# Input projection of a hybrid SSD and attention layer: seven Strassen products summed in three PSUM banks in place of seven

## The chip, the cores and the metric

The kernel runs on one core of one Trainium2 chip. The metric is the device time of one execution in microseconds (us). The core's engines work side by side, each through its own queue in order: TensorE (PE in the profile, its weight loads PEld), VectorE (DVE), ScalarE (ACT), GpSimd (POOL), and SyncE (SP), which here only issues transfers.

## The reference, cut to what matters

One decoder layer over 1024 tokens and 1024 channels. The normalised input `h` goes through one wide input projection, and its columns feed a Mamba-2 (SSD) branch, a causal attention branch with a forget gate, and two gates. The branches are projected, gated, summed and projected once more.

```python
h = _rmsnorm(x, norm_w) * (1.0 + scale[:, None, :]) + shift[:, None, :]
proj = jnp.einsum("bsd,de->bse", h, w_in)
z_ssm, xbc, dt_raw, q, k, v, z_att, f_logit, g_logit = jnp.split(proj, offsets, axis=-1)
y_ssm = _ssd_branch(z_ssm, xbc, dt_raw, ...)      # silu(conv(xbc)), decay sums, states, norm
y_att = _fox_branch(q, k, v, z_att, f_logit, b_f)
g_ssm, g_att = jnp.split(jax.nn.sigmoid(g_logit + b_gate), N_BRANCHES, axis=-1)
merged = g_ssm * (y_ssm @ w_proj_ssm) + g_att * (y_att @ w_proj_att)
x = x + gate[:, None, :] * (merged @ w_out)
return _rmsnorm(x, final_norm_w)
```

The change touches the columns of `w_in` that give `z_ssm`, `xbc`, `z_att` and 12 of the 16 blocks of 128 columns of `g_logit`: 38 blocks of 128 columns, worked off as 19 pairs.

## The kernel before, in words

`h` is kept transposed (channels on the partitions). Every float32 product is made of three single-pass matmuls: each operand is split into a rounded part (hi) and a remainder (lo), and hi*hi + hi*lo + lo*hi are added in PSUM. A split of a weight tile is a cast on ScalarE (line 102) and a subtraction on GpSimd (line 103).

Stages in time: start-up (`h` itself, the first three gate blocks), one block of values with the dt and forget columns, the sums of `h` that Strassen's scheme needs (`t_forms`), the decay sums (`dt_chain`), then the 19 slab pairs (some 120 to 540 us of the span), then the SSD stage with the rest of the projection as filling, the attention, and three more projections.

A slab pair (`c_pair`, lines 459 to 518) computes two blocks of 128 output channels for all 1024 tokens by Strassen's scheme in Winograd's form: seven products f1 to f7 in place of eight. Each product is 12 matmuls of 128x512 (four k blocks by three terms) into a PSUM bank of 128x512 float32. There are eight banks, three under the tag `mm` and five under `pp`. The weights of a pair come as four raw tiles by DMA (buffers: four, shared with other loads). VectorE makes the sums S1, S2, A11-A21 and S4 (lines 477 to 480). Then seven splits follow.

The products are added up outside TensorE. With P1 to P7 the products in the order f1, f6, f7, f5, f4, f2, f3, before the change:

- P1 is copied to SBUF as x1 (ScalarE, line 503)
- VectorE makes u2 = P6 + x1 (504), u3 = P7 + u2 (505), u4 = P5 + u2 (507), and adds in the bank P5 + u3 (508), P4 + u3 (511), P2 + x1 (514), P3 + u4 (517)
- the four banks with results are evacuated by the functions of the two slabs: a tanh on ScalarE for a gate (line 186), a tanh and a VectorE multiply for z (524, 525), a ScalarE copy into a padded tile for the convolution (534)

After a pair of convolution blocks, VectorE runs five instructions of 128x1024 for each of the two blocks (lines 538, 541, 544, with a tanh on ScalarE, line 543, before the last), and the result is stored (line 545). Convolution pairs are numbers 1, 3, 5, 7 and 9 of the 19, counted from 0. Between the pairs stand side jobs by the table `WPREP`: `w_sums` (four more raw tiles, VectorE sums at lines 586 and 587, GpSimd at 588 and 589, stores), and `out_gate` (32 VectorE instructions in all, lines 558 and 561).

The order on each engine is not written out by hand. The framework schedules the instructions on a model of the engines, by program order as priority, and then each queue is fixed. A queue is first in, first out: an instruction that waits holds up everything behind it. All transfers stand in SP's queue.

## Time and profile before

| | |
|---|---|
| three timed runs | 1295.77, 1300.94, 1301.15 us; median 1300.94 us |
| span of the profiled execution | 1298.8 us |
| time of the profiled execution around its span | not listed apart; the span is 2.1 us under the median |
| PE busy | 1204.0 us, 93% |
| DVE busy | 986.1 us, 76% |
| POOL, ACT busy | 775.3 us, 589.6 us |
| matmuls | 6206 |
| moved by DMA | 219.69 MB |

The busy time of an engine is an average over stages. Whether an engine binds in a stage is read from windows of that stage: how many matmuls start in a window, what TensorE's clock was, and what TensorE waited for where it stood idle. The granted clock has two levels, 1.2 and 2.4 GHz; the profile gives it as a share of full speed, averaged over a window.

### The profile page before, as it was taken

What the parts mean: (1) busy time and instruction counts of PE and PEld (TensorE: products, weight loads), DVE (VectorE), ACT (ScalarE), POOL (GpSimd) and SP (SyncE); (2) the same over time, 40 slices, a digit from 0 to 9 for tenths busy, and PEclk for the clock granted to TensorE, in tenths of its full rate; (3) what the DMA queues carried; (4) which work ended last, traced back from release to release, by engine and by line L of the source; (5) the groups of instructions that cost most, each with busy time, mean ns of one, the idle gap of its engine ahead of it and who ended that gap; (6) DMA issues with size and microseconds to landing.
All of it is one profiled execution on the core that took longest, in us unless ns stands there. A gap on an engine that the chain in (4) does not pass through costs nothing. (4 is left out here: it accounts for less than half of the span.)

```text
span 1298.8 us, 18747 instructions
## 1 busy us (share of the span) xinstructions
PE 1204.0 (93%) x6206; PEld 998.6 (77%) x6206; DVE 986.1 (76%) x1673; ACT 589.6 (45%) x1184; POOL 775.3 (60%) x644
## 2 busy tenths in 40 slices
PE   4897999999978999999998999999999899999896
PEld 3686788777766888899877888888888787878684
DVE  6979777787799565259889854545666968999997
ACT  5543333333342322567666633444456463444354
POOL 3267556475665565457887857435446645687666
PEclk9998899999989999999999999999998999999998
DMA  8432433633565566753744548623236618756143
GB/s 345 155 125 72 167 114 130 210 114 114 186 231 191 186 219 226 234 163 119 230 120 155 195 164 299 212 84 116 72 132 202 199 53 318 245 169 192 51 119 140
DMA packets 100669, 219.69 MB, mean 169 GB/s; under 512 B 11434, under 2 KB 19036, under 8 KB 99548
## 3 DMA queue, kind: packets, MB, share of 16 engines
q1 hardware_dynamic: 100572, 218.50, 50.4%
q8 instruction: 49, 0.80, 0.2%
q14 instruction: 48, 0.39, 0.1%
HBM read 154.85 MB, written 63.61 MB: 168 GB/s over the span
## 5 line engine op out<-in xcount | busy, mean ns | idle before, releaser
L103 POOL TENSOR_TENSOR wl<-wr,wh 128x512 fp32r<-128x512 f32 (+1 forms) x188 | 284.5, 1523 | 137.1 <-ACT wh L102 129.6
L102 ACT CAST wh<-wr 128x512 fp32r<-128x512 f32 (+1 forms) x214 | 129.7, 618 | 161.3 <-DMA wr<-w_c 51.7
L103 POOL TENSOR_TENSOR sl<-sr,sh 128x512 fp32r<-128x512 f32 x57 | 91.2, 1607 | 79.1 <-ACT sh L102 59.5
L116 PE MATMUL mm<-hl,wh 128*128 128x512 f32 x288 | 117.9, 409 | 2.9 <-DVE hl L307 2.9
L115 PE MATMUL mm<-hh,wh 128*128 128x512 f32 x288 | 116.6, 410 | 4.3 <-ACT wh L102 2.0
L117 PE MATMUL mm<-hh,wl 128*128 128x512 f32 x288 | 117.0, 407 | 0.0
L140 PE MATMUL mm<-wh,hh 128*128 128x256 f32 (+1 forms) x256 | 74.8, 294 | 3.9 <-DVE tmp L348 3.9
L102 ACT CAST sh<-sr 128x512 fp32r<-128x512 f32 x57 | 34.1, 619 | 97.1 <-DVE sr L478 77.9
L141 PE MATMUL mm<-wl,hh 128*128 128x256 f32 (+1 forms) x256 | 74.6, 292 | 0.0
L142 PE MATMUL mm<-wh,hl 128*128 128x256 f32 (+1 forms) x256 | 74.4, 291 | 0.0
L1014 ACT ACTIVATE pr<-pr,sm 128x1024 f32<-128x1024 f32 (+3 forms) x64 | 49.9, 780 | 51.5 <-DVE sm L1013 43.9
L1017 POOL TENSOR_SCALAR pr<-pr,sm 128x1024 f32<-128x1024 f32 (+3 forms) x64 | 49.3, 772 | 38.1 <-DVE sm L1016 31.8
L1009 DVE CUSTOM_DVE_ANT_0 pr<-lg,fb 128x512 f32<-128x512 f32 (+1 forms) x96 | 51.6, 551 | 25.1 <-PE lg L1008 14.6
L115 PEld LDWEIGHTS mm<-hh,wh 128*128 128x128 f32 x288 | 55.4, 194 | 16.2 <-ACT wh L102 2.4
L116 PEld LDWEIGHTS mm<-hl,wh 128*128 128x128 f32 x288 | 56.0, 194 | 15.3 <-DVE hl L307 3.9
L117 PEld LDWEIGHTS mm<-hh,wl 128*128 128x128 f32 x288 | 55.9, 194 | 11.3
L1000 POOL TENSOR_SCALAR_AFFINE_SELECT fb<-fb 128x128 f32<-128x128 f32 x64 | 20.6, 323 | 70.1 <-DVE sm L1009 57.2
L1033 DVE TENSOR_TENSOR ptl<-tp,pth 128x512 fp32r<-128x512 f32 (+1 forms) x80 | 50.1, 632 | 15.0 <-ACT pth L1032 14.1
L1032 ACT CAST pth<-tp 128x512 fp32r<-128x512 f32 (+1 forms) x80 | 42.4, 544 | 41.8 <-PE tp L1029 32.8
L684 ACT ACTIVATE ab<-ab,acs 128x128 f32<-128x128 f32 x128 | 41.2, 391 | 28.9 <-DMA ab<-a_scr 28.8
L140 PEld LDWEIGHTS mm<-wh,hh 128*128 128x128 f32 x256 | 49.3, 193 | 5.1 <-DVE tmp L348 4.6
L103 POOL TENSOR_TENSOR m<-ab,m 128x512 fp32r<-128x512 f32 x32 | 47.2, 1475 | 7.2 <-ACT m L102 6.8
(394 smaller groups left out, 3989.3 us busy)
## 6 DMA issues: line engine op xcount, KB each, us to landing
wr<-w_c SPq DMA_DIRECT2D x116, 256.0 KB, 3.6
wa<-w_ada SPq DMA_DIRECT2D x8, 1024.0 KB, 11.4
g_scr<-gt SPq DMA_DIRECT2D x16, 512.0 KB, 3.9
ab<-a_scr SPq DMA_DIRECT2D x32, 256.0 KB, 3.8
gt<-g_scr SPq DMA_DIRECT2D x32, 256.0 KB, 3.2
wr<-w_ps SPq DMA_DIRECT2D x28, 256.0 KB, 2.7
wr<-w_pa SPq DMA_DIRECT2D x28, 256.0 KB, 3.0
wr<-so SPq DMA_DIRECT2D x28, 256.0 KB, 2.7
```

The costliest lines, as they stand in the source:

```text
L102: A.copy(out=hi[:, :n], in_=raw[:, :n])
L103: eng.tensor_tensor(out=lo[:, :n], in0=raw[:, :n], in1=f32(hi[:, :n]), op=ALU.subtract)
L115: PE.matmul(ps, lhsT=hi[:, cs], rhs=xh[k][:, hs], start=(k == 0), stop=False)
L116: PE.matmul(ps, lhsT=hi[:, cs], rhs=xl[k][:, hs], start=False, stop=False)
L117: PE.matmul(ps, lhsT=lo[:, cs], rhs=xh[k][:, hs], start=False, stop=(k == 7))
L140: PE.matmul(o, lhsT=xh[k][:, ts], rhs=hi[:, cs], start=(k == 0), stop=False)
L141: PE.matmul(o, lhsT=xh[k][:, ts], rhs=lo[:, cs], start=False, stop=False)
L142: PE.matmul(o, lhsT=xl[k][:, ts], rhs=hi[:, cs], start=False, stop=(k == 7))
L1009: V.tensor_tensor_reduce(out=pr[:, n0:n1], in0=lg[:, :n1 - n0], in1=fb[:, n0:n1], op0=ALU.add, op1=ALU.min, scale=1.0, scalar=BIG, accum_o ...
L1014: A.activation(out=pr[:, :n], in_=pr[:, :n], func=AF.Exp, scale=-1.0, bias=sm[:, 0:1], accum_out=sm[:, 1:2])
L1017: G.tensor_scalar(out=pr[:, :n], in0=pr[:, :n], scalar1=sm[:, 1:2], scalar2=0.5, op0=ALU.mult, op1=ALU.mult)
L1033: V.tensor_tensor(out=ptl[:, :w], in0=tp[:, :w], in1=f32(pth[:, :w]), op=ALU.subtract)
```

## The change

The seven products of a pair now take three banks. `prod` gets an optional bank: given one, none of its 12 matmuls starts a new sum, and they add to what stands there.

- bank a: P1; copied to x1; then P2 is added by TensorE: this is the first result
- bank b: P6; VectorE adds x1 in place (line 509); copied to u2 by ScalarE (510); then P7 is added by TensorE; copied to u3 by ScalarE (513); then P4 is added: the second result
- bank d: P5; VectorE writes P5 + u3 to an SBUF tile c22 (516), which is the third result, and adds u2 in place (517); then P3 is added: the fourth result

So VectorE's seven additions become three, ScalarE's one copy becomes three, and four additions are done by matmuls that were there before. The number of matmuls is the same. The products are now issued as f1, f6, f5, f7, f2, f4, f3, and the splits as f1, f6, f5, f7, f2, f4, f3. The evacuation of the third result reads SBUF, not PSUM. Comments are removed throughout the file, so lines from 499 on move by one to four.

```diff
@@ -480,42 +480,46 @@
             f1 = a_form(a11)
             f6 = s_form(s2)
+            f5 = s_form(s1)
             f7 = a_form(a21)
-            f5 = s_form(s1)
+            f2 = a_form(a12)
             f4 = a_form(a22)
-            f2 = a_form(a12)
             f3 = s_form(s4)
 
-            def prod(f, xs, k0, hf):
-                ps = bank()
+            def prod(f, xs, k0, hf, ps=None):
+
+                first, ps = ps is None, bank() if ps is None else ps
...
-                    PE.matmul(ps, lhsT=f[0][:, w], rhs=xh[:, hs], start=(k == 0), stop=False)
...
+                    PE.matmul(ps, lhsT=f[0][:, w], rhs=xh[:, hs], start=(first and k == 0), stop=False,
+                              skip_group_check=True)
...
-            x1, u2, u3, u4 = pe_tile(), pe_tile(), pe_tile(), pe_tile()
-            A.copy(out=x1, in_=prod(f1, h, 0, 0))
-            V.tensor_tensor(out=u2, in0=prod(f6, ttb, 0, 1), in1=x1, op=ALU.add)
-            V.tensor_tensor(out=u3, in0=prod(f7, tta, 0, 1), in1=u2, op=ALU.add)
-            ps = prod(f5, tta, 0, 0)
-            V.tensor_tensor(out=u4, in0=ps, in1=u2, op=ALU.add)
-            V.tensor_tensor(out=ps, in0=ps, in1=u3, op=ALU.add)
-            evac_b(hi, ps)
-            ps = prod(f4, ttb, 0, 0)
-            V.tensor_tensor(out=ps, in0=ps, in1=u3, op=ALU.add)
-            evac_b(lo, ps)
-            ps = prod(f2, h, 4, 0)
-            V.tensor_tensor(out=ps, in0=ps, in1=x1, op=ALU.add)
-            evac_a(lo, ps)
-            ps = prod(f3, h, 4, 1)
-            V.tensor_tensor(out=ps, in0=ps, in1=u4, op=ALU.add)
-            evac_a(hi, ps)
+
+            x1, u2, u3, c22 = pe_tile(), pe_tile(), pe_tile(), pe_tile()
+            pa_ = prod(f1, h, 0, 0)
+            A.copy(out=x1, in_=pa_)
+            pb = prod(f6, ttb, 0, 1)
+            V.tensor_tensor(out=pb, in0=pb, in1=x1, op=ALU.add)
+            A.copy(out=u2, in_=pb)
+            pd = prod(f5, tta, 0, 0)
+            prod(f7, tta, 0, 1, pb)
+            A.copy(out=u3, in_=pb)
+            prod(f2, h, 4, 0, pa_)
+            evac_a(lo, pa_)
+            V.tensor_tensor(out=c22, in0=pd, in1=u3, op=ALU.add)
+            V.tensor_tensor(out=pd, in0=pd, in1=u2, op=ALU.add)
+            prod(f4, ttb, 0, 0, pb)
+            evac_b(lo, pb)
+            evac_b(hi, c22)
+            prod(f3, h, 4, 1, pd)
+            evac_a(hi, pd)
```

Three places show how the scheduled order moves. The numbers behind names are buffer numbers; `cv` and `xp` are the convolution's tiles, `sr` sums of weights, `gb` the out_gate row.

VectorE, the end of convolution pair 9, before (`mm_3139`, `mm_3155`, `pp_3170`, `pp_3185` are four products of pair 10):

```order
L505 TENSOR_TENSOR pe_3095<-mm_3125,pe_3094 128x512
L541 SCALAR_TENSOR_TENSOR cv_3008<-xp_2848,cols_80,cv_3008 128x1024
L507 TENSOR_TENSOR pe_3096<-mm_3139,pe_3094 128x512
L544 SCALAR_TENSOR_TENSOR cv_3000<-xp_2846,cv_3000 128x1024
L508 TENSOR_TENSOR mm_3139<-mm_3139,pe_3095 128x512
L511 TENSOR_TENSOR mm_3155<-mm_3155,pe_3095 128x512
L586 TENSOR_TENSOR sr_3380<-wr_3374,wr_3376 128x512
L544 SCALAR_TENSOR_TENSOR cv_3008<-xp_2848,cv_3008 128x1024
L514 TENSOR_TENSOR pp_3170<-pp_3170,pe_3093 128x512
L587 TENSOR_TENSOR sr_3381<-sr_3380,wr_3372 128x512
L517 TENSOR_TENSOR pp_3185<-pp_3185,pe_3096 128x512
```

The same place on VectorE now (`mm_3066` is bank d of pair 10, `mm_3211` bank b of pair 11):

```order
L545 SCALAR_TENSOR_TENSOR cv_2940<-xp_2792,cols_80,cv_2940 128x1024
L545 SCALAR_TENSOR_TENSOR cv_2948<-xp_2794,cols_80,cv_2948 128x1024
L545 SCALAR_TENSOR_TENSOR cv_2940<-xp_2792,cols_80,cv_2940 128x1024
L545 SCALAR_TENSOR_TENSOR cv_2948<-xp_2794,cols_80,cv_2948 128x1024
L590 TENSOR_TENSOR sr_3308<-wr_3302,wr_3304 128x512
L548 SCALAR_TENSOR_TENSOR cv_2940<-xp_2792,cv_2940 128x1024
L591 TENSOR_TENSOR sr_3309<-sr_3308,wr_3300 128x512
L548 SCALAR_TENSOR_TENSOR cv_2948<-xp_2794,cv_2948 128x1024
L516 TENSOR_TENSOR pe_3036<-mm_3066,pe_3035 128x512
L517 TENSOR_TENSOR mm_3066<-mm_3066,pe_3034 128x512
L509 TENSOR_TENSOR mm_3211<-mm_3211,pe_3193 128x512
```

The additions of the pair in flight stood between the convolution's instructions; now they stand behind them, and the addition that bank b of pair 11 needs is the last.

ScalarE at the same place, before:

```order
L543 ACTIVATE xp_2848<-cv_3008 128x1024
L503 COPY pe_3259<-pp_3263 128x512
L102 CAST wh_3432<-wr_3417 128x512
L186 ACTIVATE gt_3049<-mm_3139,cols_80 128x512
L186 ACTIVATE gt_3049<-mm_3155,cols_80 128x512
L186 ACTIVATE gt_3048<-pp_3170,cols_80 128x512
```

ScalarE at the same place now:

```order
L547 ACTIVATE xp_2794<-cv_2948 128x1024
L513 COPY pe_3035<-pp_3051 128x512
L507 COPY pe_3193<-mm_3197 128x512
L102 CAST wh_3360<-wr_3345 128x512
L510 COPY pe_3194<-mm_3211 128x512
L186 ACTIVATE gt_2988<-pp_3037,cols_80 128x512
L186 ACTIVATE gt_2989<-pp_3051,cols_80 128x512
```

The copy of u2 of pair 11 (line 510) stands behind a cast of a freshly loaded raw tile, in the place where the gate evacuations of pair 10 stood.

TensorE, where product f7 of pair 5 ends, before (f5 follows, into another bank):

```order
L495 MATMUL pp_2216<-tha3_1134,wh_2164 128x512
L496 MATMUL pp_2216<-tla3_1135,wh_2164 128x512
L497 MATMUL pp_2216<-tha3_1134,wl_2165 128x512
L495 MATMUL pp_2230<-tha0_1062,sh_2168 128x512
L496 MATMUL pp_2230<-tla0_1063,sh_2168 128x512
```

TensorE at the end of product f7 of pair 5 now:

```order
L496 MATMUL mm_2172<-tha3_1134,wh_2138 128x512
L498 MATMUL mm_2172<-tla3_1135,wh_2138 128x512
L499 MATMUL mm_2172<-tha3_1134,wl_2139 128x512
L496 MATMUL mm_2172<-thb0_1064,wh_2146 128x512
L498 MATMUL mm_2172<-tlb0_1065,wh_2146 128x512
```

Here f4 follows f7 in the same bank with nothing between, so the copy of u3 must be made between two matmuls. In the other 18 pairs 10 to 30 matmuls of other products stand between f7 and f4, and 21 to 67 between f6 and f7 in all 19.

## Rows read from the trace of the kernel before

**Rows 1.** The head of the profile page: the span, and busy time, share and instructions of TensorE and VectorE.

```profile
span 1298.8 us, 18747 instructions
...
PE 1204.0 (93%) x6206; PEld 998.6 (77%) x6206; DVE 986.1 (76%) x1673; ACT 589.6 (45%) x1184; POOL 775.3 (60%) x644
```

**Rows 2.** Stretches of 50 us: length, then busy us of each engine with the number of instructions, TensorE's clock, the DMA share and GB/s.

```profile
100.00:150.00 50.00, 41.69 (x169) 33.29 (x167) 47.03 (x68) 17.86 (x34) 33.31 (x23) 0.84 0.25 78
...
150.00:200.00 50.00, 50.00 (x217) 40.57 (x216) 34.01 (x38) 17.54 (x28) 29.75 (x20) 1.00 0.44 149
...
250.00:300.00 50.00, 44.43 (x186) 34.10 (x184) 34.96 (x44) 16.00 (x28) 30.23 (x18) 1.00 0.45 152
300.00:350.00 50.00, 46.24 (x189) 36.33 (x190) 38.07 (x43) 21.18 (x37) 32.75 (x21) 0.97 0.40 134
350.00:400.00 50.00, 42.78 (x174) 34.23 (x173) 48.95 (x57) 15.51 (x27) 31.07 (x19) 0.90 0.61 205
400.00:450.00 50.00, 44.86 (x185) 35.41 (x184) 35.78 (x56) 15.32 (x28) 25.68 (x19) 0.97 0.57 192
450.00:500.00 50.00, 50.00 (x217) 40.54 (x216) 31.97 (x45) 16.17 (x30) 33.93 (x26) 1.00 0.60 207
```

**Rows 3.** What TensorE waited for from 240 to 450 us: line and bank, releaser, us in total, times, longest.

```profile
PE mm L495 <- ACT gt L186: 7.2, 1, 7.2
PE mm L495 <- DVE zt L525: 5.1, 1, 5.1
PE pp L495 <- ACT sh L102: 3.0, 2, 2.2
PE mm L495 <- ACT sh L102: 1.9, 1, 1.9
```

**Rows 4.** Shorter stretches, columns as in rows 2.

```profile
250.00:260.00 10.00, 6.86 (x27) 4.56 (x26) 5.15 (x8) 4.97 (x10) 4.56 (x4) 1.00 0.50 155
...
300.00:310.00 10.00, 7.69 (x25) 5.85 (x26) 7.64 (x9) 5.78 (x11) 8.63 (x6) 0.83 0.30 86
...
370.00:380.00 10.00, 3.23 (x15) 2.29 (x13) 9.89 (x13) 0.92 (x2) 6.35 (x4) 0.79 0.96 331
380.00:390.00 10.00, 9.55 (x30) 7.64 (x31) 9.13 (x16) 6.33 (x12) 4.43 (x4) 0.70 0.94 346
...
410.00:420.00 10.00, 4.86 (x14) 3.30 (x13) 9.96 (x18) 3.91 (x7) 4.33 (x3) 0.84 0.29 106
420.00:430.00 10.00, 10.00 (x42) 7.75 (x42) 2.63 (x5) 1.66 (x3) 4.03 (x4) 0.99 0.42 133
...
350.00:410.00 60.00, 52.78 (x218) 42.36 (x217) 58.80 (x72) 18.27 (x31) 37.31 (x23) 0.91 0.65 217
```

**Rows 5.** Instructions in order of time around the longest wait: start, us, engine, line; in brackets the idle time before and its releaser.

```profile
348.65 3.22 DVE L538 TENSOR_SCALAR cv<-xp,cols 128x1024 f32<-128x1024 f32 x2 [1.50 <-ACT xp L534]
...
373.80 1.15 DVE L587 TENSOR_TENSOR sr<-sr,wr 128x512 f32<-128x512 f32 x1
...
376.84 0.62 ACT L102 CAST wh<-wr 128x512 fp32r<-128x512 f32 x1 [7.18 <-DMA wr<-w_c]
...
379.70 1.27 ACT L186 ACTIVATE gt<-mm,cols 128x512 f32<-128x512 f32 x2 [2.25 <-DVE gb L561]
380.44 0.79 PE L495 MATMUL mm<-thb,wh 128*128 128x512 f32 x1 [7.22 <-ACT gt L186]
```

**Rows 6.** Groups of VectorE instructions from 150 to 540 us: line, shapes, count, busy us, mean ns, idle before.

```profile
L541 DVE SCALAR_TENSOR_TENSOR cv<-xp,cols,cv 128x1024 f32<-128x1024 f32 x30 | 49.9, 1688 | 0.0
L561 DVE SCALAR_TENSOR_TENSOR gb<-wga,cols,gb 128x256 f32<-128x256 f32 x28 | 21.7, 776 | 1.0 <-DMA wga<-w_gate 0.6
L480 DVE TENSOR_TENSOR sr<-wr,sr 128x512 f32<-128x512 f32 x17 | 19.8, 1165 | 4.0 <-POOL sl L103 2.6 <-DMA wr<-w_c 1.3
L544 DVE SCALAR_TENSOR_TENSOR cv<-xp,cv 128x1024 f32<-128x1024 f32 x10 | 15.7, 1577 | 0.0
L477 DVE TENSOR_TENSOR sr<-wr 128x512 f32<-128x512 f32 x17 | 15.1, 889 | 36.8 <-DMA wr<-w_c 27.1 <-issue 9.6
L587 DVE TENSOR_TENSOR sr<-sr,wr 128x512 f32<-128x512 f32 x10 | 14.0, 1401 | 0.3 <-DVE sr L586 0.2
L538 DVE TENSOR_SCALAR cv<-xp,cols 128x1024 f32<-128x1024 f32 x10 | 13.3, 1371 | 5.5 <-ACT xp L534 5.5
...
L478 DVE TENSOR_TENSOR sr<-sr,wr 128x512 f32<-128x512 f32 x17 | 11.7, 686 | 0.8 <-DVE sr L477 0.2
...
L586 DVE TENSOR_TENSOR sr<-wr 128x512 f32<-128x512 f32 x10 | 7.6, 759 | 8.1 <-POOL sl L103 3.1 <-DMA wr<-w_pa 2.7 <-issue 1.6
...
L508 DVE TENSOR_TENSOR pp<-pp,pe 128x512 f32<-128x512 f32 x11 | 7.6, 687 | 0.0
```

**Rows 7.** Groups of ScalarE instructions from 150 to 540 us, columns as in rows 6.

```profile
L102 ACT CAST wh<-wr 128x512 fp32r<-128x512 f32 x73 | 43.4, 617 | 67.8 <-DMA wr<-w_c 49.5 <-PE pp L496 11.4 <-PE mm L497 2.2
L102 ACT CAST sh<-sr 128x512 fp32r<-128x512 f32 x51 | 30.4, 619 | 88.9 <-DVE sr L478 73.9 <-DVE sr L480 7.0 <-PE mm L496 4.8
...
L503 ACT COPY pe<-pp 128x512 f32<-128x512 f32 x12 | 7.0, 585 | 2.1 <-PE pp L497 2.1
```

**Rows 8.** One group of matmuls by its line: shortest, median and longest duration in ns, first and last start.

```profile
L495 PE MATMUL pp<-hh,wh x92: 387/392/801, 148.8 to 533.9; 128*128 128x512 f32 x92
```

**Rows 9.** ScalarE's cast ahead of the gap at 250 to 258 us, in order of time.

```profile
250.45 0.62 ACT L102 CAST wh<-wr 128x512 fp32r<-128x512 f32 x1 [8.42 <-DMA wr<-w_c]
```

More of the change, by code (lines that the diff above doesn't have):

```diff
@@ L494, in prod @@
                     xh, xl = xs[k0 + k]
-                    PE.matmul(ps, lhsT=f[0][:, w], rhs=xh[:, hs], start=(k == 0), stop=False)
-                    PE.matmul(ps, lhsT=f[0][:, w], rhs=xl[:, hs], start=False, stop=False)
-                    PE.matmul(ps, lhsT=f[1][:, w], rhs=xh[:, hs], start=False, stop=(k == 3))
+                    PE.matmul(ps, lhsT=f[0][:, w], rhs=xh[:, hs], start=(first and k == 0), stop=False,
+                              skip_group_check=True)
+                    PE.matmul(ps, lhsT=f[0][:, w], rhs=xl[:, hs], start=False, stop=False, skip_group_check=True)
+                    PE.matmul(ps, lhsT=f[1][:, w], rhs=xh[:, hs], start=False, stop=(k == 3), skip_group_check=True)
                 return ps
```

## The prediction

> **What bounds the kernel now.** I read the head of the page first: TensorE is busy for 93% of a span of 1298.8 us, VectorE for 76% [rows 1]. So only what TensorE loses can be won. The stretches of 50 us show where it loses [rows 2]. Fully fed it starts 217 matmuls of 128x512 in 50 us (150 to 200 and 450 to 500 us), one in 0.2304 us. From 250 to 450 us it starts 186, 189, 174 and 185: 134 fewer than 4 x 217, or 30.9 us. Of that, 21.7 us are idle and the rest is the slower clock of the starts after a gap. From 100 to 150 us it is not fed either, while VectorE is busy for 47.0 of 50 us.
>
> What it waits for in these 200 us [rows 3]: a bank not yet evacuated (gate evacuation 7.2 us, z evacuation 5.1 us) and casts of the weight sums (3.0 and 1.9 us). I split the 30.9 us by shorter stretches [rows 4], at 43.4 matmuls per 10 us. 370 to 390 us holds 45 in place of 86.8: 9.6 us. 410 to 430 us holds 56: 7.1 us. Together 16.7 us, and 14.2 us for the rest, of which 3.8 us lie at 250 to 260 us (27 matmuls). VectorE is busy for 58.8 of the 60 us from 350 on: the two long waits are its backlog. In order of time [rows 5]: convolution pair 9 starts on VectorE at 348.65, and L587, on which a raw weight buffer depends, starts at 373.80 and ends at 374.95; the load behind it holds a ScalarE cast until 376.84, and the gate evacuation behind that cast ends TensorE's wait of 7.22 us at 380.44. The wait at 250 to 258 us is another: there the cast itself waited 8.42 us for its load [rows 9], behind two sets of `w_sums` in SP's queue.
>
> **The change, part by part.** VectorE loses four additions of 0.687 us [rows 6] in each of 19 pairs: 52.2 us. ScalarE gains two copies of 0.585 us [rows 7] in each: 22.2 us. A pair takes TensorE 84 x 0.2304 = 19.35 us, as before; the added terms ride on matmuls that are there anyway. VectorE loses 2.75 us per pair: in the 60 us from 350, 3.1 pairs, so 8.5 us, and a load of 98% comes down to 84%. The ScalarE copies are hidden beside TensorE as long as ScalarE does not stand at a wait; it is busy for about a third.
>
> What is added on the path is a new kind of wait. Before, TensorE waited for the other engines only when it wanted a bank back, some five products later. Now f7 waits for an addition and a copy in its own bank, and f4 for a copy. Without queueing these cost 0.69 + 0.59 us and 0.59 us, each with 0.16 us of drain (0.39 us duration, 0.23 us spacing [rows 8]). The scheduler has put 21 to 67 matmuls between f6 and f7 (4.8 us or more) and 10 to 30 between f7 and f4 (2.3 us or more), taken from the neighbouring pairs. Only pair 5 has none between f7 and f4: 0.85 us with 0.1 us estimated for the handover.
>
> So what counts is queueing. I work out the tight places.
>
> Pair 11, whose f7 needs the last VectorE instruction behind convolution pair 9. Before, that stretch took 26.3 us (348.65 to 374.95). It held six additions that go or move (4.1 us), and L477 to L480, of which all but the last now stand ahead of it (889 + 2 x 686 ns [rows 6], 2.3 us). That leaves 19.9 us. Ahead of it 1.0 us for the end of a matmul and the copy of the last block, behind it L544 (1.6), two additions (1.4), the added one (0.7) and the copy (0.6): 25.2 us. Between f3 of pair 9 and f7 of pair 11 the order has 107 matmuls, 24.7 us. The other way, by load and cast, is 1.0 + 19.9 + 1.9 (374.95 to 376.84) + 0.6 + 0.6 = 24.0 us. I take 1.0 us lost where 9.6 us were.
>
> Pair 3, behind convolution pair 1: 2 x 1.371 + 6 x 1.688 + 2 x 1.577 = 16.0 us of convolution, 3.4 us of weight sums, three additions 2.1, copies and drain 1.6: 23.1 us against 104 matmuls, 24.0 us. Pair 5, behind convolution pair 3: 16.0, two additions 1.4, two sums of `w_sums` 2.2 [rows 6], four z multiplies at the length of an addition 2.7, the added one 0.7, copies and drain 1.6: 24.6 against 107 matmuls, 24.7 us. I take 0.5 us each.
>
> The out_gate instructions (28 of 0.776 us, 21.7 us [rows 6]) fall on pairs 10 to 13. Two pairs of TensorE are 38.7 us. I take 2.5 us there, nearest to what remains of 7.1 us when 5.5 us of additions in two pairs are gone.
>
> The weight waits: the 3.8 us at 250 us hang on SP's queue and stay. Of the other 10.4 us half stays: ScalarE waited 73.9 us for the weight sums of VectorE [rows 7], which now come earlier, but the raw buffers still bound them. For u2 and u3 copies held in ScalarE's queue behind casts that wait for a load (49.5 us of such waits in all, [rows 7]) I take 2.0 us.
>
> The sum of what the pairs lose. Before, from 250 to 450 us: 16.7 + 3.8 + 10.4 = 30.9 us. After: 1.0 (pair 11) + 2.5 (out_gate) + 3.8 (load at 250 us) + 5.2 (other weight waits) + 1.0 (f7 of pairs 3 and 5) + 0.9 (f4 of pair 5) + 2.0 (copies behind casts) = 16.4 us. That is 14.5 us won. At the start of the stage the first pair's f7 comes behind the decay sums on VectorE, which TensorE waits for anyway: 0.5 us lost. The later stages compute the same, though the scheduler deals their filling out somewhat differently; I count 0, from -5 to +5. Net 14.0 us. The sum is made against the profiled execution (span 1298.8 us); its time around the span is not listed, and the median of the runs is 2.1 us above it. 1300.9 - 14 = 1287 us.
>
> Bounds of the unknown terms: the tight places can cost 0 (the 16.7 us then go whole) or 4 us each (some half of the worst wait of before, 7.2 us); the copies behind casts 0 to 8.4 us, the longest such wait [rows 9].
>
> **The rivals.**
>
> First, the wait changes its name. The two long waits ended on ScalarE's queue [rows 5], and the u2 copy of pair 11 stands exactly where the gate evacuation stood, behind the same cast. If the load comes no earlier, TensorE stops at f7 in place of at the bank: the 16.7 us stay for the most part. For it: the raw buffer depends on L587 at the end of the convolution as before. Against it: that end comes 6 us earlier. 16.7 + 3.8 + 5.2 + 3.9 for the small new waits is 29.6 us, a gain of about 1 us: 1300 us.
>
> Second, slower: the chain in one bank. Before, VectorE could be late by some five products, 14 us, before TensorE stood still; now by 21 to 36 matmuls, 5 to 8 us, less 1.4 us for addition and copy. A convolution stretch is even with TensorE to within a microsecond, so from about 3 us of lateness each of five convolution pairs and two out_gate pairs stops TensorE for 3 us. A short gap also costs clock: at 300 us 2.3 idle us lost 18.4 matmuls, 4.2 us [rows 4], so 1.9 us on top. 7 x 4.9 = 34 us, against some 22 us of old losses that go: 12 us slower, 1313 us. Against it: the mean durations used hold GpSimd's disturbance already, and VectorE's load falls.
>
> The Trainium skill speaks for this rival (Perfetto Trace Analysis, section Matmuls): independent groups should rotate through different banks, so that evacuation runs beside the next group's matmuls. Here three products share a bank with an evacuation between each two. The trace of before agrees with the rule as far as it goes: with seven banks per pair TensorE did not lose a matmul from 150 to 200 us [rows 2]. By the bare rule, with nothing to fill in, each pair would lose 1.4 + 0.8 us, 42 us in all; the scheduled order, which fills from the next pair, is why I do not take it.
>
> Third, more than forecast. With VectorE relieved the weight sums are always early, and all but the 3.8 us go, some of the start-up's loss too: 30 us, 1270 us. Against it: five convolution stretches are still even with TensorE.
>
> **How the numbers follow.** Forecast 0.62, with its own range 1277 to 1296; the wait renamed 0.18; slower 0.13; more 0.07. The range goes from 1270, the larger gain, to 1308, into the slower case but not to its whole price. About 0.5% (6.5 us) is what a measurement of this kernel can tell from no change: under 1294.4 us, over 1307.4 us. Faster: 0.07 and 0.57 of the forecast's 0.62, 0.64. Same: 0.05 and 0.16 of the renamed wait, 0.21. Slower: 0.13 and 0.02, 0.15.
>
> **What would show it.** In the profile of the changed kernel: 217 matmuls per 50 us again between 350 and 450 us; VectorE at 80 to 88% there; the waits for gate and z evacuations gone from TensorE's list, and in their place small ones, 0.5 to 3 us, at f7 for the u2 copy and at f4 for the u3 copy; ScalarE about 22 us busier, VectorE about 52 us less. The gap behind the two `w_sums` (near 250 us) still there. I am wrong if f7 waits for the u2 copy in sum over 12 us, if the granted clock falls in the convolution pairs, or if the gain of the stage is lost again in the SSD stage.

## The result, and the profile after

The changed kernel takes 1307.61 us (median of 20 runs, 1298.65 to 1312.64) against 1301.06 us for the kernel before in the same session (20 runs): a ratio of 1.0044, 95% interval 1.0031 to 1.0056. It is slower by 0.44%, some 6 us; the forecast was 14 us faster. The profiled execution took 1310.21 us with a span of 1308.5 us, 9.7 us longer than the span of before [rows 1]. The medians differ by 6.6 us, so the two traced executions show some 3 us more than the change costs on average; what follows divides up their 9.7 us.

The head of its page, and stretches with the columns of rows 2 (at 500 us a stretch of 37 us, since the pairs of the kernel before end at 537 us):

```profile
span 1308.5 us, 18695 instructions
...
PE 1207.9 (92%) x6206; PEld 998.4 (76%) x6206; DVE 934.3 (71%) x1597; ACT 609.8 (47%) x1222; POOL 776.4 (59%) x644
```

```profile
100.00:150.00 50.00, 37.92 (x161) 29.86 (x162) 44.81 (x66) 17.61 (x35) 31.03 (x21) 0.86 0.24 76
150.00:200.00 50.00, 47.53 (x204) 38.33 (x203) 26.97 (x29) 18.07 (x33) 31.18 (x21) 0.99 0.52 158
200.00:250.00 50.00, 50.00 (x213) 40.47 (x213) 32.73 (x39) 22.25 (x36) 26.96 (x16) 0.98 0.43 145
250.00:300.00 50.00, 45.36 (x182) 35.35 (x181) 31.49 (x36) 19.03 (x33) 31.93 (x19) 0.93 0.54 177
300.00:350.00 50.00, 46.75 (x196) 37.64 (x195) 32.27 (x32) 22.73 (x39) 34.41 (x22) 0.97 0.46 159
350.00:400.00 50.00, 48.04 (x207) 38.18 (x206) 42.69 (x48) 19.38 (x33) 27.48 (x17) 1.00 0.50 173
400.00:450.00 50.00, 43.99 (x183) 33.60 (x182) 29.55 (x46) 14.52 (x27) 25.02 (x18) 1.00 0.57 189
450.00:500.00 50.00, 46.26 (x194) 35.73 (x193) 25.51 (x35) 17.17 (x32) 30.95 (x23) 1.00 0.66 226
...
500.00:537.00 37.00, 33.39 (x128) 25.82 (x127) 14.81 (x19) 14.33 (x27) 24.74 (x19) 0.91 0.56 180
```

Two stretches of the kernel before that rows 2 leave out:

```profile
200.00:250.00 50.00, 50.00 (x217) 40.56 (x216) 40.16 (x51) 16.42 (x28) 25.80 (x17) 1.00 0.52 178
...
500.00:537.00 37.00, 36.38 (x156) 28.73 (x155) 18.31 (x25) 13.50 (x23) 24.88 (x19) 1.00 0.69 227
```

The matmul counts say where the time went. A row counts every matmul that runs in its stretch, so one that runs over an edge counts on both sides, here as in the prediction. From 250 to 450 us the rows count 768 in place of 734 [rows 2]: 34 more, 7.8 us won at 0.2304 us each (31 more, 7.1 us, by one row over the whole 200 us, shown further down). Everywhere else in the stage they count fewer: 8 from 100, 13 from 150, 4 from 200, 23 from 450 and 28 from 500 us, together 76, or 17.5 us. The difference, 42 matmuls, is 9.7 us, as much as the whole change of the span. VectorE is indeed 52 us less busy and ScalarE 20 us more.

The first transposing matmul of the SSD stage shows that little is gained or lost later. First the kernel before, then the changed one; the two numbers ahead of the semicolon are its first and last start in us.

```profile
L692 PE MATMUL xp<-ident,xs x64: 270/272/476, 552.5 to 739.8; 128*128 128x128 f32 x64
```

```profile
L696 PE MATMUL xp<-ident,xs x64: 270/273/331, 563.6 to 754.0; 128*128 128x128 f32 x64
```

SSD starts 11.1 us later, and the program ends 9.7 us later. The loss lies in the pairs; 1.4 us come back behind them.

What TensorE waited for in the changed kernel, 120 to 550 us, with the columns of rows 3:

```profile
PE pp L496 <- ACT pe L513: 4.8, 2, 3.0
PE pp L499 <- POOL wl L103: 4.6, 3, 3.2
PE mm L496 <- ACT pe L513: 3.9, 2, 3.2
PE mm L496 <- ACT gt L186: 3.6, 1, 3.6
PE mm L496 <- DVE mm L517: 3.4, 2, 2.5
PE pp L496 <- DVE pp L517: 2.9, 3, 1.4
...
PE pp L496 <- ACT pe L510: 0.7, 2, 0.4
PE mm L496 <- ACT pe L510: 0.7, 1, 0.7
```

In the changed file L513 is the u3 copy (P4 waits for it), L517 the addition of u2 to P5's bank (P3 waits for it), L510 the u2 copy (P7 waits for it). Together 8.7 + 6.3 + 1.4 = 16.4 us. The two long waits of [rows 3], 12.3 us, are gone, and 16.4 us have come back as twelve waits of 0.3 to 3.2 us, inside the banks. So the wait did change its name. Four of the twelve, 5.3 us, stand where the kernel before was fully fed: one of 2.5 us at 198 us, and three from 472 to 502 us.

How such a small wait comes about, in order of time, with the columns of rows 5 (changed kernel, 488 to 504 us):

```profile
488.17 0.59 ACT L510 COPY pe<-pp 128x512 f32<-128x512 f32 x1 [7.16 <-DVE pp L509]
...
497.51 0.69 DVE L477 TENSOR_TENSOR sr<-wr 128x512 f32<-128x512 f32 x1 [1.80 <-DMA wr<-w_c]
...
499.02 1.14 ACT L102 CAST sh<-sr 128x512 fp32r<-128x512 f32 x2 [4.03 <-DVE sr L478]
...
501.63 0.57 ACT L513 COPY pe<-pp 128x512 f32<-128x512 f32 x1
...
502.25 0.50 PE L496 MATMUL pp<-thb,wh 128*128 128x512 f32 x1 [1.83 <-ACT pe L513]
...
503.37 0.63 PE L496 MATMUL pp<-thb,wh 128*128 128x512 f32 x1
```

Read it from the end. P4 (of pair 16) stands for 1.83 us for the u3 copy. The copy is late because ScalarE has casts of weights ahead of it, and those waited 4.03 us for a sum on VectorE, which waited for a load. In the kernel before, an evacuation behind those casts could be late without harm: its bank was wanted some products later. Now the next product of the bank stands directly behind it. The 0.63 us of the last row is the lower clock of the matmuls just after the gap (granted clock 0.91 from 500 to 537 us). That price is not paid at every such wait: from 350 to 500 us, where eight of the twelve lie, one of them 3.0 us long, the granted clock stays at 1.00.

### The profile page after: what moved, and what is told of

It is laid out like the page before. It is cut to its first block, busy times and chain, and to the rows that moved or that the text cites. A ratio compares the mean times of both kernels' runs of the same rounds, so it can differ in the third digit from the quotient of the medians.

```text
span 1308.5 us, 18695 instructions
## 1 busy us (share of the span) xinstructions
PE 1207.9 (92%) x6206; PEld 998.4 (76%) x6206; DVE 934.3 (71%) x1597; ACT 609.8 (47%) x1222; POOL 776.4 (59%) x644
## 5 line engine op out<-in xcount | busy, mean ns | idle before, releaser
L103 POOL TENSOR_TENSOR wl<-wr,wh 128x512 fp32r<-128x512 f32 (+1 forms) x188 | 279.8, 1498 | 143.9 <-ACT wh L102 137.7
L103 POOL TENSOR_TENSOR sl<-sr,sh 128x512 fp32r<-128x512 f32 x57 | 85.6, 1514 | 60.2 <-ACT sh L102 47.3
L1013 DVE CUSTOM_DVE_ANT_0 pr<-lg,fb 128x512 f32<-128x512 f32 (+1 forms) x96 | 51.8, 551 | 23.9 <-PE lg L1012 14.3
L1037 DVE TENSOR_TENSOR ptl<-tp,pth 128x512 fp32r<-128x512 f32 (+1 forms) x80 | 50.1, 632 | 16.7 <-ACT pth L1036 16.5
L545 DVE SCALAR_TENSOR_TENSOR cv<-xp,cols,cv 128x1024 f32<-128x1024 f32 x30 | 53.6, 1831 | 0.0
```

Source lines behind the costliest of these rows:

```text
L103: eng.tensor_tensor(out=lo[:, :n], in0=raw[:, :n], in1=f32(hi[:, :n]), op=ALU.subtract)
L545: V.scalar_tensor_tensor(out=v, in0=xp[:, i:i + S], scalar=cols[:, R_CW + 10 * i + j:R_CW + 10 * i + j + 1], in1=v, op0=ALU.mult, op1=ALU.add)
L1013: V.tensor_tensor_reduce(out=pr[:, n0:n1], in0=lg[:, :n1 - n0], in1=fb[:, n0:n1], op0=ALU.add, op1=ALU.min, scale=1.0, scalar=BIG, accum_o ...
L1037: V.tensor_tensor(out=ptl[:, :w], in0=tp[:, :w], in1=f32(pth[:, :w]), op=ALU.subtract)
```

## The experiments

Each run was compared with the kernel before on the same chip; the number is the ratio with its 95% interval. The theories, with letters as the expectations use them:

- **A, the chain:** products that wait for a sum in their own bank cost the time.
- **B, ScalarE's queue:** the added copies hold up the casts behind them.
- **C, the order:** the new order of splits and products costs it.
- **V, VectorE:** the two long waits of before are VectorE's backlog (the premise of the prediction).
- **D, raw buffers:** the four buffers for raw weights set the pace of the stage.
- **E, shared tiles:** the gate's weights sit in the buffers that the evacuations need.

### Parts of the change, one at a time

```diff
# e1, against the changed kernel: its order, the sums of before (cut to P6)
-V.tensor_tensor(out=pb, in0=pb, in1=x1, op=ALU.add)
-A.copy(out=u2, in_=pb)
+V.tensor_tensor(out=u2, in0=prod(f6, ttb, 0, 1), in1=x1, op=ALU.add)
...
# e2, against e1
-pa_ = prod(f2, h, 4, 0)
-V.tensor_tensor(out=pa_, in0=pa_, in1=x1, op=ALU.add)
+prod(f2, h, 4, 0, pa_)
# e3, against e1
+V.tensor_tensor(out=pb, in0=pb, in1=x1, op=ALU.add)
+A.copy(out=u2, in_=pb)
...
+prod(f7, tta, 0, 1, pb)
+A.copy(out=u3, in_=pb)
...
+prod(f4, ttb, 0, 0, pb)
...
# e4, against e1
+V.tensor_tensor(out=c22, in0=pd, in1=u3, op=ALU.add)
+V.tensor_tensor(out=pd, in0=pd, in1=u2, op=ALU.add)
...
+prod(f3, h, 4, 1, pd)
```

> The new order of the weight splits and of the products (P1, P6, P5, P7, P2, P4, P3), but the sums of the kernel before: seven banks per pair, each product in its own, seven additions on VectorE, no added copy. Theory A (the chain: products wait for the sum that stands in their bank): the order alone costs nothing, 1301 us, 1298 to 1304. Theory B (ScalarE's queue: the added copies wait at its head and hold up the weight casts behind them): 1301 us as well. Theory C (the order: weight buffers are freed in a worse sequence, so weights come late whatever the sums do): 1306 to 1309 us, nearly all that the changed kernel lost, with the waits for weights near 500 to 530 us in the trace.

> As the run before, and P2 alone is accumulated in P1's bank: one addition of 0.69 us per pair goes (13 us of VectorE), no copy is added, and the copy that P2 waits for lies five products back. Theories A and B: faster than the kernel before, 1293 to 1298 us, since nothing new stands in the way and the backlog of VectorE shrinks by a quarter of what the change took. Theory C: 1302 to 1306 us.

> The new order, and P6, P7 and P4 alone share a bank, with the addition in place and the copies u2 and u3 on ScalarE; P2 and P3 have banks of their own and are added by VectorE as before. VectorE loses two additions per pair (26 us), ScalarE gains two copies (22 us). Theory A: slower than the kernel before, 1306 to 1312 us, with TensorE waiting at P4 for the u3 copy (8 us in sum) and small gaps at P7. Theory B: also 1306 to 1312 us, but the u2 copies stand some 35 to 40 us at the head of ScalarE's queue and TensorE's waits are for weights (wl, sl, sh, wh), not for the copies. Theory C: as the run of the order alone, 1306 to 1309 us.

> The new order, and P3 alone is accumulated in P5's bank, so that it must wait for the addition of u2 there; one addition of VectorE per pair goes, no copy is added. Theory A: a small loss or none against the run of the order alone, 1299 to 1305 us: the waits at P3 for VectorE (6 us in the changed kernel) against 13 us less work on VectorE. Theory B: faster, 1294 to 1298 us, as nothing is added to ScalarE. Theory C: 1304 to 1308 us.

Measured: the order alone 1.0003 (0.9985 to 1.0020); with bank a 0.9998 (0.9977 to 1.0018); with bank b 1.0045 (1.0021 to 1.0069); with bank d 1.0007 (0.9994 to 1.0020). C is out. Bank a takes 13 us of work off VectorE and adds hardly a wait (0.6 us for the x1 copy), and still gains nothing, which is the first sign against V: TensorE's waits for gate and z evacuations fall from 15.7 us in the kernel before to 9.9, but those for weights rise from 9.2 to 13.1. Bank b alone costs as much as the whole change, which spoke for A. In its trace the long waits are at P7:

```profile
PE pp L496 <- ACT pe L509: 14.7, 7, 4.0
...
PE mm L496 <- ACT pe L509: 3.3, 2, 2.2
```

L509 is the u2 copy there: 18.0 us, where the changed kernel loses 1.4 us at P7 and 15.0 us at P4 and P3. So it isn't one link that is too short. Bank d alone has its waits too, at P3 (L514 is the addition of u2 there):

```profile
PE mm L496 <- DVE mm L514: 11.5, 2, 6.7
PE pp L496 <- DVE pp L514: 5.2, 4, 2.0
```

In that trace the last matmul of the pairs starts 9.8 us later than in the kernel before, but the program ends only 1.7 us later. So the time of e4 does not say that its pairs lose nothing; why 8 us come back behind them was not tested (nine matmuls of a later block stand among its last products, some 2 us).

### Copies on another engine, copies alone, no addition in the chain

```diff
# e7, against the changed kernel
-A.copy(out=u2, in_=pb); A.copy(out=u3, in_=pb)
+V.tensor_copy(out=u2, in_=pb); V.tensor_copy(out=u3, in_=pb)
# e8, against the changed kernel (P1 goes to bank b as well, P2 to its own, and the order changes; cut)
-V.tensor_tensor(out=pb, in0=pb, in1=x1, op=ALU.add)
+prod(f6, ttb, 0, 1, pb)
...
# e10, against the kernel before, for P6 and for P7
+A.copy(out=u4, in_=ps)
```

> The changed kernel with the copies u2 and u3 on VectorE in place of ScalarE: ScalarE has the work of the kernel before again, VectorE gets 38 copies back (some 22 to 26 us). Theory B (copies at the head of ScalarE's queue, 39 us of waiting there, hold up the casts): back to 1299 to 1303 us. Theory A (P7, P4 and P3 stand too close behind their sums): 1305 to 1311 us, the waits at P7 and P4 now named after VectorE, and longer behind a convolution. Theory D: 1305 to 1309 us.

> P1 and P6 are accumulated in one bank, so that u2 = P1 + P6 stands there without an addition; u2 and u3 are copied by ScalarE as in the changed kernel, P7 and P4 follow in that bank; P2 gets a bank of its own and x1 is added there by VectorE. As many additions and copies as the changed kernel, but no product of the chain waits for VectorE; only P3 does. Products in the order P1, P5, P6, P2, P7, P3, P4. Theory A with VectorE as the late link (the addition ahead of the u2 copy stands behind convolutions): 1298 to 1303 us, ScalarE's 39 us in front of the u2 copies gone. Theory A without it (any two products of one bank too close): 1305 to 1311 us. Theory B: 1298 to 1303 us. Theory D: 1303 to 1308 us, as the raw buffers are the same.

> The kernel before with two more copies of 128x512 per pair on ScalarE, of the banks of P6 and P7 into the tile that u4 is written to later; no product waits for them, no bank is shared. ScalarE gets the 22 us of the changed kernel. Theory A (the shared bank is what costs): 1300 to 1304 us. If ScalarE's added work costs by itself: 1305 to 1309 us.

Measured: copies on VectorE 1.0096 (1.0073 to 1.0119), worse, with 14.3 us of waits at P4 that now carry VectorE's name; P1 and P6 in one bank 1.0059 (1.0039 to 1.0079), no better than the change; the copies alone, with nobody waiting, 0.9998 (0.9983 to 1.0014). B is out as a theory of ScalarE's load: 22 us more on ScalarE cost nothing. Together with e3, where TensorE waits 18.0 us for u2 copies, that says what costs: that TensorE waits for the copy. Taking VectorE's addition out of the chain (e8) did not help either: the waits moved to casts (16.4 us, where the kernel before has 5.2), to P4 (4.8 us) and to the last link of bank d (5.1 us).

### What VectorE's relief is worth, and the raw buffers

e9 leaves all seven additions out of the kernel before. e5 gives the kernel before a fifth raw buffer, e6 gives it to the changed kernel, e12 adds bank a to e5 in the old order, e17 is e9 with the fifth buffer.

```diff
# e5, against the kernel before (cut)
+if len(raws) % 5 == 0:
+    return pa.tile([P, 512], F32, tag="wr5", bufs=1, name="wr5")
...
-tag="pe", bufs=4
+tag="pe", bufs=3
...
+b21 = ev("b21")[:, :512]
...
-V.tensor_tensor(out=u4, in0=ps, in1=u2, op=ALU.add)
+V.tensor_tensor(out=u2, in0=ps, in1=u2, op=ALU.add)
```

> The kernel before, with a fifth raw weight buffer in the stage of the slab pairs: every fifth load of a slab pair or of the weight sums goes into a buffer of its own. Its 2 KB per partition come from the tiles of the sums (three in place of four, u4 written over u2; one tile of the stage's start is taken from another pool). Theory D (the four raw buffers set the pace: SP's queue waits some 110 to 120 us for GpSimd's remainders and some 68 us for VectorE's sums to free them, in the kernel before, with P2 alone in place, and in the changed kernel alike): 1283 to 1294 us, SP's waits for raw buffers down by a quarter or more. Theory V (VectorE's backlog, as in the prediction): within 4 us of the kernel before. Theories A and B say nothing of it.

> The changed kernel with the same fifth raw buffer (the sum c22 written over u3). Theory D: the loads come earlier, and then the relief of VectorE can show: at or below the kernel before with a fifth buffer, 1283 to 1294 us. Theory A (the chain in bank b is what costs): the chain's waits stay, 1303 to 1309 us. Theory B: 1303 to 1307 us.

> The kernel before with all seven additions of a slab pair left out (each product is evacuated as it is; P6 and P7 are not read), so the part left out is the sums of the seven products, and the output is not the layer's. VectorE loses 19 x 7 x 0.69 = 91 us, nearly twice what the changed kernel takes from it, and nothing is added anywhere. Theory V (the two long waits are VectorE's backlog, the premise of the prediction): 1270 to 1282 us, the waits for gate and z evacuations gone. Theory D (four raw weight buffers set the pace): 1290 to 1299 us, the waits for weights (9 us in the kernel before) still there or larger.

> The kernel before in its own order, with the fifth raw buffer and with P2 accumulated in P1's bank: one addition per pair less on VectorE (13 us). With the fifth buffer alone TensorE still waits 22 us for gate and z evacuations and under 1 us for weights. If the backlog of VectorE is what is left: 1283 to 1288 us, below the run with the fifth buffer alone. If not: 1289 to 1293 us, the same as that run.

> The kernel before with all seven additions of a slab pair left out (the part left out is the sums of the seven products) and with the fifth raw buffer. If the raw buffers hid what VectorE's relief is worth: 1270 to 1280 us, far more below the fifth buffer alone (about 1291 us) than the 5.5 us that the same omission gave with four buffers. If VectorE's load in the stage is worth little whatever the buffers do: 1283 to 1290 us.

| kernel before, with | four raw buffers | five |
|---|---|---|
| the seven additions | 1 | 0.9924 (0.9902 to 0.9946), e5 |
| none of them | 0.9958 (0.9945 to 0.9972), e9 | 0.9810 (0.9782 to 0.9838), e17 |

The changed kernel with five buffers is at 1.0009 (0.9992 to 1.0026), e12 at 0.9957 (0.9944 to 0.9970).

This is the main finding. With four buffers, taking 91 us of work from VectorE gains 0.42%, 5.5 us. With five, the same omission gains 1.14 points, 14.8 us. So by these times the raw buffers hid 9.3 of 14.8 us of what a relief of VectorE is worth, and the change takes only 52 us from it. In the traces part of that difference lies behind the pairs: in the pairs, from the second on, the omission wins 7.1 us with four buffers and 11.2 us with five. In e9 two long waits stay (6.7 and 7.7 us), though no sum is made at all:

```profile
PE mm L495 <- ACT gt L186: 9.3, 2, 6.7
PE pp L561 <- DVE gb L552: 7.7, 1, 7.7
```

V as the prediction put it has fallen: with four buffers these waits are not the backlog of the sums. What e9 wins lies ahead of them: 9.0 us from 251 to 321 us (pairs 6 to 8), where the kernel before waited for weights. TensorE's waits for weights are 3.5 us in e9, where the kernel before has 9.2; D had said that they stay or grow, and missed. SP's queue shows the other side: how long its loads of the pairs and of `w_sums` stood for a raw buffer, from 120 to 540 us, freed by GpSimd's remainders (POOL wl) or VectorE's A11-A21 (DVE wr). First the kernel before, then e5 (its own line numbers: 588 and 471 are the loads).

```profile
SPq L579 <- POOL wl L103: 68.0, 27, 7.2
SPq L462 <- POOL wl L103: 51.0, 21, 7.7
SPq L579 <- DVE wr L479: 43.3, 10, 9.4
SPq L462 <- DVE wr L479: 24.6, 7, 6.7
```

```profile
SPq L588 <- POOL wl L103: 62.5, 25, 6.7
SPq L471 <- POOL wl L103: 38.2, 17, 9.5
...
SPq L588 <- DVE wr L488: 15.5, 6, 5.0
...
SPq L471 <- DVE wr L488: 10.6, 4, 4.1
```

187 us of such waits became 127 us, and TensorE's waits for weights, 9.2 us in the pairs of before, came down to 0.6 us. Some of it only changes place in the same queue: the stores of the weight sums wait 78 us in place of 44. D holds for the time and for the waits for weights. e5 also starts its pairs 5.7 us earlier (a side effect of the tile taken from another pool), but that is not its gain: 8.9 us of wait for the first pair's gate evacuation and 6.3 us for the decay sums follow, and the second pair starts at 154.5 us, where it started at 153.9. The pairs then end 9.8 us earlier. Nor do three tiles for the sums in place of four hold it up: the x1 copy waits 2.6 us once for VectorE. With the weights on time the waits for evacuations are the largest that are left, and without the sums (e17) they are gone behind the first pair. First e5, then e17, from 120 us on; the 8.9 us stand in the first pair of each:

```profile
PE mm L504 <- ACT gt L186: 11.5, 2, 8.9
PE mm L504 <- DVE zt L534: 6.4, 1, 6.4
...
PE pp L504 <- DVE zt L534: 4.5, 1, 4.5
```

```profile
PE mm L504 <- ACT gt L186: 8.9, 1, 8.9
PE pp L570 <- DVE gb L561: 7.0, 1, 7.0
```

So with five buffers the sums do hold the evacuations up, as V said of the kernel before. One thing e9 and e17 don't tell apart: without sums nothing reads P6 and P7, so two of a pair's seven banks come free at once, beside VectorE's relief. Matmuls from 250 to 450 us, in the kernel before, e5, e9 and e17, one row of each:

```profile
250.00:450.00 200.00, 178.31 (x731) 140.06 (x730) 157.75 (x196) 68.01 (x119) 119.74 (x76) 0.96 0.51 171
```

```profile
250.00:450.00 200.00, 185.96 (x770) 148.28 (x769) 165.15 (x202) 69.97 (x121) 122.14 (x80) 0.96 0.52 175
```

```profile
250.00:450.00 200.00, 183.10 (x762) 145.30 (x761) 124.31 (x136) 68.60 (x122) 116.36 (x78) 0.96 0.50 170
```

```profile
250.00:450.00 200.00, 193.01 (x823) 155.26 (x822) 131.81 (x140) 68.30 (x121) 123.22 (x83) 0.98 0.54 187
```

39 more with the buffer, 31 more without the sums, 92 more with both: more than the two together. The changed kernel has 762 in the same stretch, as many as e9. In this stretch the change won as much as leaving out every sum does.

e6 adds a fifth buffer to the changed kernel and gains a third of a per cent, where the kernel before gains three quarters. That is what A expected of it, not D. With the weights mended (0.5 us of waits for them), the waits inside the banks are the largest part of what is left, 14.4 us, and the changed kernel lies 0.85 points above e5, about 11 us. e12 missed: 13 us less on VectorE did not improve on e5 but cost 0.3 points, with 3.8 us of new waits of P2 for the x1 copy.

### Room to run ahead, and the gate's tiles

```diff
# e11, against the kernel before
-if len(banks) % 8 in (1, 2, 3):
-    return mm_tile()
# e13, e14, e15, against the kernel before, the changed one, e5
-wa = ev("wga")[:, :1024].rearrange("p (k c) -> p k c", k=4)
-SP.dma_start(out=wa, in_=t["w_gate"][g, hf])
-in0=wa[:, kk, :]
+in0=f32(hh[k])[:, :256]
# e16, against e5
-wa = ev("wga")[:, :1024].rearrange("p (k c) -> p k c", k=4)
...
+wq = raw5()[:, :512].rearrange("p (k c) -> p k c", k=2)
...
```

> The kernel before with its products rotating through five PSUM banks in place of eight, nothing else changed: TensorE may run ahead of the evacuations by some four products in place of seven. Theory A, in the form that what the chain takes away is TensorE's room to run ahead: 1306 to 1316 us, with longer waits for evacuations behind the convolutions. If room to run ahead is not what counts: 1300 to 1304 us.

> The kernel before, with the products of out_gate reading a resident tile (256 columns of the modulated input) in place of loaded gate weights: the eight loads of w_gate and their eight tiles in the pool of the evacuations go, VectorE's 32 instructions of out_gate stay as many and as large. The part changed is the gate's weights, so the output gate is not the layer's. Theory E (the four buffers shared by the gate's weights and the evacuations hold the two long waits): 1285 to 1293 us, and from 350 to 430 us no wait of TensorE above 3 us. Theory V (VectorE's load there): within 4 us of the kernel before.

> The changed kernel with the same change of the gate (the gate's weights are changed, so the output is not the layer's). Theory A (three products in one bank cost 5 to 6 us whatever else is mended): 3 to 8 us above the kernel before with the same change. If the gate's tiles had hidden the gain of the sums in place: at or below it.

> The kernel before with the fifth raw buffer and without the gate's loads and tiles (the gate's weights are changed, so the output is not the layer's). Theory E with D: the two add up, 1277 to 1284 us, and little is left of waits for evacuations (22 us with the fifth buffer alone). If E is wrong: 1289 to 1293 us.

> The kernel before with the fifth raw buffer, and the gate's weights loaded in sixteen halves into the five raw buffers in place of the buffers of the evacuations; it computes the layer. Theory E: the evacuations no longer wait for them, but the raw buffers carry sixteen more loads: 1281 to 1290 us, below the fifth buffer alone. If the raw buffers are too short for that, or E is wrong: 1290 to 1298 us.

e11: 1.0177 (1.0156 to 1.0199), as A in this form expected. The pairs begin 18.3 us later (138.2 in place of 119.8 us), behind a wait of 11.9 us for the decay sums; but in the kernel before the decay sums and 20 matmuls of the block of values fall into the first pair, so the second pair starts only 5.1 us later (159.0 in place of 153.9). The last matmul of the pairs starts 19.9 us later. So 14.8 us are lost from the second pair on, with waits of 25.1 us for gate and z evacuations and the out_gate row; the kernel before waits 13.1 us for them there. Room to run ahead does count in this stage. That the chain takes it away is not shown by this run, which takes banks away and shares none.

e13: 1.0031 (1.0017 to 1.0046). E is right for one of the two long waits. The wait of 7.2 us for a gate evacuation falls to 1.0 us; in the kernel before that evacuation starts as an out_gate instruction of VectorE ends (L561), which reads the gate's weights [rows 5]. The z wait falls too, 5.1 us to nothing, but 6.0 us of wait for weights now stand ahead of it, and with weights on time it stays (e15, below). All waits for gate and z evacuations go from 15.7 to 4.5 us. But the kernel gets slower though work was only taken away: waits for weights rise from 9.2 to 21.2 us, for instance

```profile
PE pp L495 <- ACT sh L102: 8.9, 3, 6.0
PE mm L495 <- ACT sh L102: 5.5, 3, 2.1
```

in place of 3.0 and 1.9 us [rows 3]. e14, the changed kernel with the same edit: 1.0020 (0.9999 to 1.0040), level with e13, so A's fixed price of 5 to 6 us is not upheld. e15, on top of the fifth buffer: 0.9892 (0.9871 to 0.9913), 0.3 points below e5, hardly clear of the noise and less than E expected. No gate evacuation behind the first pair holds TensorE there, but the z waits are 11.2 us, as in e5 (10.9 us). e16: 0.9997 (0.9984 to 1.0009); sixteen more loads through the raw buffers cost all that the fifth buffer had won, with one wait of 17.0 us for a cast.

### The change without bank b

```diff
# e18, against the changed kernel
-V.tensor_tensor(out=pb, in0=pb, in1=x1, op=ALU.add); A.copy(out=u2, in_=pb)
+V.tensor_tensor(out=u2, in0=prod(f6, ttb, 0, 1), in1=x1, op=ALU.add)
-prod(f7, tta, 0, 1, pb); A.copy(out=u3, in_=pb)
+V.tensor_tensor(out=u3, in0=prod(f7, tta, 0, 1), in1=u2, op=ALU.add)
...
-prod(f4, ttb, 0, 0, pb)
+pb = prod(f4, ttb, 0, 0)
+V.tensor_tensor(out=pb, in0=pb, in1=u3, op=ALU.add)
```

> The changed kernel with P6, P7 and P4 in banks of their own again, their sums made by VectorE as before, and no added copy: P2 stays accumulated in P1's bank and P3 in P5's; two of seven additions are gone (26 us of VectorE). Theory A (bank b is the cost): level with the kernel before, 1298 to 1304 us. If the cost lies in any of the waits for sums in a bank: 1304 to 1309 us.

Measured: 1.0071 (1.0044 to 1.0098). Bank b alone is not the cost: without it the kernel is no faster, and TensorE waits at P3 instead:

```profile
PE mm L496 <- DVE mm L514: 8.0, 3, 4.3
PE pp L496 <- DVE pp L514: 6.7, 3, 2.6
```

14.7 us at P3 (L514 is the addition of u2 there), where the changed kernel has 6.3. Why banks a and d together cost 0.7%, when the time of each alone cannot be told from that of the kernel before, stays open. The traces narrow it down: e4 has as much at P3, 16.7 us, and its pairs end 9.8 us later than those of before, in e18 8.6 us. The difference lies behind the pairs, where e4 wins 8 us back and e18 loses 1 us more. The parts do not add up. A possible reason, not tested, is that every edit makes the scheduler deal out another order on every queue.

## Why the prediction was wrong

**The premise, "the two long waits are its backlog".** This step failed for the kernel as it was, with four raw buffers. The sum took 16.7 us of loss as VectorE's and left 3.5 of it. From 350 to 410 us the changed kernel starts 241 matmuls where there were 218 [rows 4], and from 410 to 430 us 65 where there were 56: 32 more, 7.4 us, so 9.3 us of loss stay. So that part of the forecast came true, but not by VectorE's relief: without any addition (e9) the two rows from 350 to 450 us count 349 matmuls, where they count 359 in the kernel before and 390 in the changed one. The gate wait hung on the tiles that gate weights and evacuations share (e13). What the z wait hung on is not shown. With four raw buffers the waits for gate and z evacuations mostly go with the banks that a pair takes. Without the first pair's wait of 2.6 to 4.1 us, they are 13.1, 19.4 and 12.8 us with seven banks (before, e1, e10), 5.8 and 2.3 us with six (e2, e4), 0 and 1.0 us with five (e3, e18), none with three (e8, the changed kernel). That is a pattern over these runs, with exceptions at seven banks (e9 6.7 us, e13 2.0 us); no run changed the banks per pair alone. [Rows 5] showed the shared tile in the bracket of the gate evacuation, whose releaser is an out_gate instruction (gb L561); I read only the cast ahead of it.

**The sum of what the pairs lose, 14.5 us won from 250 to 450 us.** Measured 7.8 us won. VectorE is busy for 49.4 of the 60 us from 350 on, 82%, as forecast. The granted clock, whose fall the prediction named as a sign against it, does both: 0.93 from 250 to 300 us, where it was 1.00, and 1.00 from 350 to 400 us, where it was 0.90 [rows 2].

**"0.5 us lost" outside these stretches.** This step failed most: 17.5 us. The prediction costed the new waits only at places that already looked tight, and took the fully fed stretches as safe. There TensorE had hardly waited (0.6 us, at 520 us), because an evacuation could be late by several products. The change took this tolerance away in every pair. Of the 17.5 us, 11.8 us (51 matmuls) lie from 450 us on, where TensorE's idle time is 7.4 us: 2.8 us inside the banks, and 4.5 us for weights, which come late there as they did not before. Much of the rest is the lower clock behind the gaps from 500 us on (0.91); from 450 to 500 us the clock is 1.00. From 150 to 250 us 3.9 us are lost to one wait of 2.5 us at P3 and the clock behind it (0.99, 0.98). The 1.8 us from 100 to 150 us are the start of the stage, where no wait lies inside a bank. So the waits inside the banks are 5.3 us of the idle time out here; why the weights come late from 450 us on was not tested.

**f4 of pair 5 0.9 us, copies behind casts 2.0 us.** The mechanism was right. P4 of pair 5 waits 0.7 us, as forecast; but P4 also waits in pairs 8, 12 and 16, 8.0 us, where the sum had 2.0 us for all copies; the one at 502 us stands behind casts, as shown above. P3's wait for the addition in its bank, 6.3 us, was not in the sum.

**f7 of pairs 3, 5 and 11, 2.0 us.** Measured 1.4 us in all, in pairs 12, 15 and 16 and none in these. The bound that the prediction set itself, 12 us at f7, was not reached; the place was wrong, not the kind of wait.

**Half of the other weight waits stay.** Not halved: 9.2 us of idle time before and 9.3 us after, from the start of the pairs on. A fifth raw buffer takes them to 0.6 us (e5), and leaving out all additions to 3.5 us (e9); the relief that the change gives did not. The 2.5 us for out_gate were put down as what remains of 7.1 when 5.5 us are gone, which is 1.6 us; the sum is not wrong by much there.

**The first rival**, the wait that changes its name, described the outcome (16.4 us inside the banks for 15.7 us at them), but placed it at f7 of pair 11. **The second rival**, slower through the chain, had the direction: a gain of some old losses, lost again in small gaps, some with a clock price on top. Its price of 7 x 4.9 us was too high for one wait and blind to the number: 12 waits averaging 1.4 us. The rule of the Trainium skill that spoke for it (Perfetto Trace Analysis, section Matmuls), to rotate independent groups through different banks, agrees with e3, e8 and e18, which share banks and are slower, but not with the times of e2 and e4, which share one each at no cost that can be told from zero, though e4 waits 16.7 us inside its bank. **The third rival**, 1270 us, is near what it takes to leave out all sums and add a buffer (e17, 1276.17 us).

**Busy times** came as forecast: VectorE 52 us less, ScalarE 20 us more. They say nothing about the time.

The Trainium skill also says (Perfetto Trace Analysis, section Optimization Strategy) that repeating bubbles can mean too few buffers for the next tile. The fifth raw buffer (0.9924) agrees with it here. The fastest version that computes the layer is e5, 1291.01 us.

## What to carry to other kernels

Before giving a busy engine less to do, find out what that relief is worth, by leaving the work out; here 91 us of it were worth 5.5 us, and 14.8 us once another buffer came free. It is no upper bound: e13, where loads were only taken away, got slower. A wait put between two products of one bank is paid wherever anything upstream is late, also in stretches that show no wait now (here 5.3 of 16.4 us), so cost it over the whole stage and not at the tight places. Where queues are first in, first out and a scheduler fixes them, look for the buffer that the loads wait for.

## What the runs showed of the hardware that was not expected

VectorE's convolution products (128x1024) ran longer in the changed kernel, though it had less to do. The row of the changed kernel that answers to L541 of rows 6, now over the whole span with the same 30 instructions:

```profile
L545 DVE SCALAR_TENSOR_TENSOR cv<-xp,cols,cv 128x1024 f32<-128x1024 f32 x30 | 53.6, 1831 | 0.0
```

1831 ns on average against 1688 [rows 6], 4.3 us in all. The two traces go some way to say why. In the kernel before, 11 of the 30 have next to no GpSimd instruction beside them (under a tenth of their time), in the changed kernel 10, and each of these takes 1269 to 1276 ns. Each of the longer ones, up to 2342 ns, has GpSimd at work beside it for a third of its time or more; some beside GpSimd stay short. So, as far as the traces place GpSimd's work, they get longer only beside it. No run was made to change that.
